# Attention iterations placed among the projections and the output projection of a hybrid encoder layer

## The chip, the cores and the metric

One Trainium2 chip; the kernel runs on one NeuronCore. The metric is the device time of one execution in microseconds. The kernel before takes 3338.55 us (median of three runs, 3337.0 to 3348.45).

## The reference

One encoder layer on x of 2048 tokens by 1024, all in fp32. Cut to what matters:

```python
h = rms_norm(x, norm1_g); proj = h @ w_in            # 1024 -> 2560
hy_in, q, k, v, pool_in = split(proj)                # 768, 512, 512, 512, 256
y_hy   = hyena_mixer(hy_in, ..., hyena_filter(...))  # long convolution, by DFTs
y_na   = neighbourhood_attention(q, k, v, na_rpb)    # 8 heads of 64, window 8 x 16 on a 32 x 64 grid
y_pool = pool_mixer(pool_in, pool_w, pool_scale)     # means over 2, 4, 8, 16 tokens
mixed  = concat(rms_norm(y_hy), rms_norm(y_na), rms_norm(y_pool)) # each with its part of mix_norm_g
x = x + mixed @ w_out
x = x + expert_choice_moe(rms_norm(x, norm2_g), w_router, w_gate, w_up, w_down)  # 16 experts, 256 tokens each
return rms_norm(x, final_g)
```

## The kernel before, in words

Everything is one class, `Trunk`; `run` strings the stages together. Large products are done in a reduced fp32 format, each as three matmuls: `split` cuts an operand into a high part (ScalarE, L212) and the rest (VectorE, L213), and `mm3` (L217 to L219) multiplies high by high, high by low and low by high. Tiles come from rotating pools: a tag with `bufs=n` has n buffers, and the next tile of that tag waits for the last reader of the one whose buffer it takes. A scheduler with a simulated timeline decides the order of the instructions on each engine; each engine then runs its own list strictly in order.

**Projections** (`proj`, `prep`, `slab`). The 2048 tokens are four chunks of 512, two chunks to a half. `prep` loads a tile of 128 tokens (`x0`, 4 buffers), takes the RMSNorm (ACT L236, POOL L204 and L206, DVE L238), transposes it on TensorE (L243, 8 transposes a tile) and splits it into `hT_h`, `hT_l`. The 2560 columns are ten slabs of 256, in five groups of two; slabs 0 to 2 feed the hyena mixer, 3 and 4 are queries, 5 and 6 keys, 7 and 8 values, 9 pooling. Each half runs all five groups over its two chunks: 80 calls of `slab`, 24 matmuls of 512 columns each (48 of 256 for values). Weights come in pieces of 512 KB on SP's queue. Results go to HBM (`Ud`, `KD`, `QD`, `Vd`).

**Beside the projections**: in the first half the generator `filt` (the filter of the hyena mixer, its DFT; POOL L392 and TensorE L395 among its lines) and `bias_tables`; in the second half `hyena` (39 steps, four a slab call) and `pooling` (eight steps, from the seventh slab call on, one a call). One pooling step is a chain: load `po<-Ud` (L557, POOL's queue), sums on DVE (L548) and POOL (L562, L567), scale (L570), one matmul (L577, PSUM tag `fl`), eviction (ACT L579) into the loaded tile, store `Ypd` (L580). Its three tiles take all three buffers of the tag, so the next load waits for this store.

**Attention** (`attention`) then has PSUM to itself (`psum_b`: two banks each of `s`, `tp`, `o`). It has 16 units of four iterations, 64 in all. An iteration is `scores` (6 matmuls `s<-at_k,at_q`; DVE L768 adds the bias and takes the minimum; ACT L772 the exponential), `turn` (transposes `tp<-ident,at_s`, evicted by ACT L790 or DVE L788 into `at_p`) and `weigh` (`o<-at_p,at_v`, evicted by ACT L808). All of its TensorE instructions are recorded at L715, in `pe`, which chains each to the one before, so that their order is written out by hand. `load_wo` runs beside it: 32 loads of 128 KB of the output weight on POOL's queue (L870, `wo_raw`, 2 buffers), each multiplied by the norm's gain and split (ACT L862, DVE L863).

**Output projection** (`mix`, `out_proj`, `route`): eight chunks of 256 tokens. `mix` loads the three mixers' outputs and splits them; for each tile of 128 tokens 48 matmuls of 512 columns, the sum with x (DVE L978 into `wo_x`, 3 buffers), 8 transposes (L983), the store to `Acc`, a squared sum (ACT L988) and the router's logits. **The rest** is `top_tokens` and `experts`, which the change leaves as they are.

Of the kernel before, what the change touches and what calls it, by code (L numbers as in the profile page):

```python
# [10 lines left out]
F = mybir.dt.float32  # L11
# [142 lines left out]
def _layouts(a):  # L154
# [19 lines left out]
    w = np.ascontiguousarray(a["w_in"][0].reshape(2, 4, 128, 10, 256).transpose(3, 0, 2, 1, 4))  # L174
# [9 lines left out]
class Trunk:  # L184
# [30 lines left out]
    def mm3(self, out, lh, ll, rh, rl, start, stop):  # L215
# [6 lines left out]
    def prep(self, pool, early, chunk, out):  # L222
# [6 lines left out]
        for t in range(4):  # L229
            xt = self.sb(early, [128, D], "x0", bufs=4)  # L230
            nc.sync.dma_start(xt, x[(chunk * 4 + t) * 128:(chunk * 4 + t + 1) * 128])
            if chunk + t == 0:
                nc.sync.dma_start(self.g1, _bc(self.i["norm1_g"], D))
# [15 lines left out]
    def proj(self, pool, early):  # L249

        nc, i = self.nc, self.i
        self.g1 = self.sb(early, [128, D], "g1", bufs=1)
        ht = {}
        for _ in self.prep(pool, early, 0, ht):
            pass
        groups = ((1, 2), (0, 9), (7, 8), (5, 6), (3, 4))
        for half, group in itertools.product(range(2), groups):
            if 3 in group:
                self.copy_values(half)
            w = {}  # L260
            for s in group:
                wh, wl = [], []
                for q in range(2):
                    raw = self.sb(pool, [128, 4, 256], "w1_r", bufs=2)
                    nc.sync.dma_start(raw, self.c["w_in_t"][s, q])
                    h = self.sb(pool, [128, 4, 256], "w1_h", R, bufs=4)
                    l = self.sb(pool, [128, 4, 256], "w1_l", R, bufs=4)
                    self.split(h, l, raw)
                    wh += [h[:, d] for d in range(4)]
                    wl += [l[:, d] for d in range(4)]  # L270
                w[s] = wh, wl
            for ch in range(2):
                chunk = half * 2 + ch
                ahead = None
                if group == groups[-1] and chunk == 1 or group == groups[0] and ch == 0:
                    ahead = self.prep(pool, early, chunk + 1, ht)
                for s, m in itertools.product(group, range(2)):
                    if ahead:
                        next(ahead)
                    self.slab(pool, s, m, chunk, *w[s], *ht[chunk])  # L280
                    yield half, s

    def copy_values(self, half):

        rows = slice(half * 16, half * 16 + 16)
        for k, (c0, k0, nk) in enumerate(self.CB):
            self.nc.gpsimd.dma_start(self.Vc[k][rows], self.Vd.rearrange("(r c) n -> r c n", c=64)[rows, k0:k0 + nk])

    def slab(self, pool, s, m, chunk, wh, wl, hh, hl):
# [3 lines left out]
        if s in (7, 8):  # L293
            for t2 in range(2):
                sl = slice((m * 2 + t2) * 128, (m * 2 + t2 + 1) * 128)
                for d in range(8):
                    self.mm3(pt[:, t2 * 256:(t2 + 1) * 256], hh[:, d, sl], hl[:, d, sl],
                             wh[d], wl[d], d == 0, d == 7)
# [4 lines left out]
            nc.scalar.dma_start(dst.rearrange("(a p) n -> p a n", p=128), ev)  # L303
            return
        for d in range(8):
            self.mm3(pt, wh[d][:, m * 128:(m + 1) * 128], wl[d][:, m * 128:(m + 1) * 128],
                     hh[:, d, :], hl[:, d, :], d == 0, d == 7)
# [20 lines left out]
        else:  # L328
# [3 lines left out]
            nc.scalar.dma_start(self.Ud[r0:r0 + 128, tok], ev)  # L332


    def filt(self, pool):
# [6 lines left out]
        nc.gpsimd.dma_start(self.d2, c["dft_2"])  # L342
        nc.gpsimd.dma_start(self.d2p, c["dft_2p"].bitcast(R))
# [54 lines left out]
        for g4 in range(8):  # L398
# [4 lines left out]
            for g2 in range(2):  # L403
                ph = self.bank("fl", (128, 2, 256))
                for e in range(2):
                    k, x = g2 * 2 + e, 0 if g4 + g2 + e else 1
                    self.mm3(ph[:, e, :], self.d2p[:, 0, x], self.d2p[:, 1, x], ah[:, k, :], at[:, k, :], True, True)
# [13 lines left out]
    def hyena(self, pool):  # L421
# [5 lines left out]
        nc.gpsimd.dma_start(ph, c["par_h"])  # L427
        sw = ph[:, 0:18].rearrange("p (t k) -> p t k", k=3)
# [42 lines left out]
        for g4 in range(8):  # L471
# [6 lines left out]
            for g2 in range(2):  # L478
# [3 lines left out]
                for e in range(2):  # L482
                    k, x = g2 * 2 + e, 2 if first[e] else 0
                    nc.tensor.matmul(pz[:, e, :], lhsT=self.d2[:, x], rhs=at[:, k, :], start=True, stop=True)
# [12 lines left out]
                for e in range(2):  # L497
                    x = 3 if first[e] else 1
                    nc.tensor.matmul(pb[:, e, :], lhsT=self.d2[:, x], rhs=y[:, e, :], start=True, stop=True)
# [142 lines left out]
    def attention(self, kpool, get_pool):  # L642
# [42 lines left out]
        def load_values(u):  # L685
# [4 lines left out]
            for cb in self.QB[g * 2:g * 2 + 2]:  # L690
# [3 lines left out]
                if g:  # L694
                    if rb == 0:
                        wide[cb] = kb([128, 8, 256], f"at_vw{cb}")
                        nc.sync.dma_start(wide[cb][:, 0:4], values(0, 4, 128))
                        nc.gpsimd.dma_start(wide[cb][:, 4:8], values(512, 4, 128))
# [11 lines left out]
        mark = nc.cur_bb.bb.instructions[-1]  # L710
        self.chain = None

        def pe(op, *args, **kw):

            ins = op(*args, **kw).ins  # L715
            if self.chain is not None:
                self.tc.add_manual_dep(ins, self.chain.name,
                                       mybir.DependencyInfo(mybir.DependencyClass.NoSync, mybir.DependencyReason.DATA),
                                       reason="order of the attention")
            self.chain = ins  # L720
# [4 lines left out]
        def begin(u):  # L725
# [11 lines left out]
            if u + 1 < len(units):  # L737
                w.tabs = dict(bias)
                with self.tc.issue_after(mark):
# [681 lines left out]
```

## Time and profile before

| | |
|---|---|
| profiled execution, own time | 3335.52 us |
| its span on the core | 3333.7 us |
| median of 3 runs (lowest, highest) | 3338.55 us (3337.0, 3348.45) |
| busy in the span: PE, DVE, ACT, POOL | 96%, 57%, 46%, 11% |
| projections, filter, hyena, pooling | 0 to 600 us |
| attention, load of the output weight | 600 to 860 us |
| output projection | 860 to 1077 us |
| choice of the tokens | 1077 to 1133 us |
| experts, final norm | 1133 us to the end |

PE is TensorE's matmuls, PEld its weight loads, DVE VectorE, ACT ScalarE, POOL GpSimd, SP SyncE. A row "L715 ... x416 | 69.7, 310 | 48.0 <-ACT" says: line, engine, operation, out<-in, count, busy us, mean ns of one, idle us of the engine just before, and what ended it. Matmuls overlap, so the mean of one is a latency; its cost on a full engine comes from counts in a stretch without idle time. The bounds of the stages are where TensorE's lines change over.

### The profile page before, as it was taken

What the parts mean: (1) busy time and instruction counts of PE and PEld (TensorE: products, weight loads), DVE (VectorE), ACT (ScalarE), POOL (GpSimd) and SP (SyncE); (2) the same over time, 40 slices, a digit from 0 to 9 for tenths busy, and PEclk for the clock granted to TensorE, in tenths of its full rate; (3) what the DMA queues carried; (4) which work ended last, traced back from release to release, by engine and by line L of the source; (5) the groups of instructions that cost most, each with busy time, mean ns of one, the idle gap of its engine ahead of it and who ended that gap; (6) DMA issues with size and microseconds to landing.
All of it is one profiled execution on the core that took longest, in us unless ns stands there. A gap on an engine that the chain in (4) does not pass through costs nothing.

```text
span 3333.7 us, 45008 instructions
## 1 busy us (share of the span) xinstructions
PE 3190.7 (96%) x18002; PEld 2690.7 (81%) x18002; DVE 1902.3 (57%) x2555; ACT 1518.9 (46%) x2004; POOL 363.5 (11%) x468
## 2 busy tenths in 40 slices
PE   8999999678999599999999999999999999999998
PEld 6887898456787488888888888888888888888886
DVE  5124557356676665565665655656556565565565
ACT  4124422366332355454454544545445445454464
POOL 2212212222111000000000000000000000000012
PEclk9999999888999699999999999999999999999999
DMA  6677687875553457666576665665656656666596
GB/s 223 213 258 233 204 307 267 229 199 155 169 165 130 138 193 212 196 200 203 198 208 200 198 203 195 210 202 194 211 193 204 202 197 209 195 192 203 188 299 231
DMA packets 421782, 685.50 MB, mean 206 GB/s; under 512 B 27378, under 2 KB 323042, under 8 KB 421190
## 3 DMA queue, kind: packets, MB, share of 16 engines
q1 hardware_dynamic: 362742, 530.74, 49.4%
q0 software_dynamic: 29552, 106.09, 11.0%
q10 hardware_dynamic: 29280, 45.81, 4.0%
q8 instruction: 141, 2.31, 0.3%
q14 instruction: 67, 0.55, 0.0%
HBM read 573.86 MB, written 119.03 MB: 208 GB/s over the span
## 4 chain that ended last, share of the span: by engine, by line
PE 86%; DMA 6%; issue 4%; DVE 2%; ACT 1%; SPq 1%; POOL 0%; POOLq 0%; ACTq 0%; DVEq 0%
PE mm L1193 27%; PE mm L1195 13%; PE mm L217 13%; PE mm L219 13%; PE mm L218 13%; DMA at_t<-Ce 2%; PE tp L1162 1%; DMA mo_xg<-Hr,mo_ix 1%; DMA wo_raw<-in_w_out 1%; DMA QD<-e 1%; PE tp L715 1%; PE o L715 1%; DMA at_q<-QD 0%; PE tp L395 0%; PE fl L521 0%
## 5 line engine op out<-in xcount | busy, mean ns | idle before, releaser
L1193 PE MATMUL mm<-mo_xx,mo_wh 128*128 128x512 f32 x4096 | 1446.3, 398 | 0.6 <-DVE mo_xx L213 0.6
L213 DVE TENSOR_TENSOR mo_wl<-mo_raw,mo_wh 128x2048 fp32r<-128x2048 f32 x384 | 879.7, 2291 | 790.3 <-ACT mo_wh L212 790.2
L1195 PE MATMUL mm<-mo_xx,mo_wl 128*128 128x256 f32 x4096 | 1151.7, 281 | 0.0
L212 ACT ACTIVATE mo_wh<-mo_raw 128x2048 fp32r<-128x2048 f32 x384 | 735.4, 1915 | 702.8 <-issue 323.4
L1193 PEld LDWEIGHTS mm<-mo_xx,mo_wh 128*128 128x128 f32 x4096 | 771.3, 188 | 185.2 <-DVE mo_xx L213 1.0
L1195 PEld LDWEIGHTS mm<-mo_xx,mo_wl 128*128 128x128 f32 x4096 | 775.5, 189 | 0.7
L218 PE MATMUL mm<-mo_wl,mo_hh 128*128 128x512 f32 x1024 | 398.4, 389 | 0.0
L217 PE MATMUL mm<-mo_wh,mo_hh 128*128 128x512 f32 x1024 | 398.1, 389 | 0.0
L219 PE MATMUL mm<-mo_wh,mo_hl 128*128 128x512 f32 x1024 | 396.0, 389 | 0.0
L219 PEld LDWEIGHTS mm<-mo_wh,mo_hl 128*128 128x128 f32 x1024 | 192.2, 188 | 40.2
L217 PEld LDWEIGHTS mm<-mo_wh,mo_hh 128*128 128x128 f32 x1024 | 192.2, 188 | 40.1
L218 PEld LDWEIGHTS mm<-mo_wl,mo_hh 128*128 128x128 f32 x1024 | 192.3, 188 | 39.3
L1226 POOL DMA_INDIRECT Acc<-mo_y,mo_ix x30 | 69.5, 2315 | 1395.3 <-ACT mo_y L1225 1279.0
L217 PE MATMUL mm<-hT_h,w_h 128*128 128x512 f32 x512 | 204.6, 402 | 2.1 <-ACT hT_h L212 2.1
L218 PE MATMUL mm<-hT_l,w_h 128*128 128x512 f32 x512 | 205.1, 401 | 0.0
L219 PE MATMUL mm<-hT_h,w_l 128*128 128x512 f32 x512 | 204.0, 398 | 0.0
L1201 ACT ACTIVATE mo_s<-mo_s 128x512 f32<-128x512 f32 x128 | 81.0, 633 | 235.8 <-DVE mo_s L1198 235.6
L1198 DVE TENSOR_TENSOR mo_s<-mo_s,mm 128x512 f32<-128x512 f32 x256 | 174.0, 680 | 0.0
L1197 ACT ACTIVATE mo_s<-mm 128x512 f32<-128x512 f32 x256 | 147.7, 577 | 0.0
L217 PEld LDWEIGHTS mm<-hT_h,w_h 128*128 128x128 f32 x512 | 96.0, 188 | 25.8 <-ACT hT_h L212 2.8
L218 PEld LDWEIGHTS mm<-hT_l,w_h 128*128 128x128 f32 x512 | 96.1, 188 | 25.4 <-issue 2.8
L212 ACT ACTIVATE mo_hh<-mo_s 128x512 fp32r<-128x512 f32 x128 | 79.9, 624 | 78.7 <-DVE mo_s L1202 78.7
(307 smaller groups left out, 3614.8 us busy)
## 6 DMA issues: line engine op xcount, KB each, us to landing
mo_raw<-in_w_gate SPq DMA_DIRECT2D x128, 1024.0 KB, 5.4
mo_raw<-in_w_up SPq DMA_DIRECT2D x128, 1024.0 KB
mo_raw<-in_w_down SPq DMA_DIRECT2D x128, 1024.0 KB, 4.9
w_r<-c_w_in_t SPq DMA_DIRECT2D x40, 512.0 KB, 7.2
x<-in_x SPq DMA_DIRECT2D x16, 512.0 KB, 9.8
Ud<-e ACTq DMA_DIRECT2D x32, 256.0 KB, 4.4
Hd<-t ACTq DMA_DIRECT2D x32, 256.0 KB, 6.0
t<-Hd SPq DMA_DIRECT2D x16, 512.0 KB, 7.0
```

Source lines behind the costliest of these rows:

```text
L212: self.nc.scalar.activation(hi, src, AF.Copy)
L213: self.nc.vector.tensor_tensor(lo, src, hi.bitcast(F), op=OP.subtract)
L217: mm(out, lhsT=lh, rhs=rh, start=start, stop=False)
L218: mm(out, lhsT=lh, rhs=rl, start=False, stop=False)
L219: mm(out, lhsT=ll, rhs=rh, start=False, stop=stop)
L715: ins = op(*args, **kw).ins
L1193: nc.tensor.matmul(pt[:, m].rearrange("p k t -> p (k t)"), lhsT=w[:, d, ms], rhs=xx[:, d].rearrange("p k t -> p (k t)"), start=d == 0, sto ...
L1195: nc.tensor.matmul(pt[:, m, 1], lhsT=wlo[:, d, ms], rhs=xx[:, d, 0], start=False, stop=d == 7)
L1197: nc.scalar.activation(a, pt[:, :, 1], AF.Copy)
L1198: nc.vector.tensor_tensor(a, a, pt[:, :, 0], op=OP.add)
L1201: nc.scalar.activation(s, s, AF.Silu)
L1226: nc.gpsimd.indirect_dma_start(out=self.Acc, out_offset=off, in_=y, in_offset=None, compute_op=OP.add)
```

## The change

The projections run in three **phases**: phase 0 takes four slabs (1, 2, 0, 9) of the second half, phase 1 all ten slabs of the first half, one slab at a time, phase 2 the other six (7, 5, 3, 8, 6, 4) of the second half. Chunks 2 and 3 are therefore normalised and transposed twice. Weight pieces are 256 KB; in phase 2 they come on POOL's queue. `filt` runs beside phase 0 and the first two slabs of phase 1, `hyena` beside phase 1 from slab 0 on, and `pooling` when `hyena`'s steps are used up.

In phase 2 the matmuls join attention's chain (`held`). A slab call gives the control back three times; from the 16th time on one or two attention steps go between two parts (57 parts, 85 of 130 steps). The other 45 steps (22 iterations) follow with `load_wo` (two steps of it for each attention step), and then with `mix` and `out_tiles` for one tile of 128 tokens after every sixth step. The last tiles go in pairs as before. Attention's PSUM is now one bank `s`, two `tp`, one `o`, two `mm`, one `x`; `weigh` goes ahead of `scores`. A tile of one has one buffer for each of its `mx_h`, `wo_hh`, `wo_x`.

```diff
     def mm3(self, out, lh, ll, rh, rl, start, stop, held=False):
         mm = self.nc.tensor.matmul
+        if held:
+            mm = lambda *a, **k: self.pe(self.nc.tensor.matmul, *a, **k)
...
+    PHASES = ((1, ((1, 2), (0, 9))),
+              (0, ((1,), (2,), (0,), (9,), (7,), (5,), (3,), (8,), (6,), (4,))),
+              (1, ((7,), (5,), (3,), (8,), (6,), (4,))))
...
+                    for q in range(4):
+                        raw = self.sb(wpool, [128, 2, 256], "w1_r", bufs=wbufs[0])
+                        (nc.gpsimd if ph == 2 else nc.sync).dma_start(raw, self.c["w_in_t"][s, q])
+                        h = self.sb(wpool, [128, 2, 256], "w1_h", R, bufs=wbufs[1])
...
+                        again = ph == 2 or ph == 1 and gi
+                        g1 = self.sb(late, [128, D], "g1", bufs=1) if again and ph == 1 else None
+                        ahead = self.prep(pool, late if again else early, ahead, ht, g1, 1 if again else 4)
...
                 for d in range(8):
                     self.mm3(pt[:, t2 * 256:(t2 + 1) * 256], hh[:, d, sl], hl[:, d, sl],
-                             wh[d], wl[d], d == 0, d == 7)
+                             wh[d], wl[d], d == 0, d == 7, held)
+                    if t2 * 8 + d in (4, 9):
+                        yield t2
...
+                if len(line) > 2:
+                    weigh(line.pop(0))
                 line.append(scores(unit, j, hp))
+                yield
                 if len(line) > 1:
                     turn(line[-2])
-                if len(line) > 2:
-                    weigh(line.pop(0))
                 yield
...
+                if ph == 1:
+                    if kpool is None and part == 2:
+                        more = steps(hy, 4)
+                        if n > 27:
+                            more = steps(side, 1) or more
...
+                    psa = psum("psum_b", s=1, tp=2, o=1, mm=2, x=1)
+                    at = self.attention(kpool, attn_pool)
+                    next(at)
+                    n = 0
+                if n > 15:
+                    for _ in range(1 + n % 2):
+                        next(at)
+            proj.release()
+            wo = sbuf("wo", left)
+            self.out_weights(wo)
+            weights = self.load_wo(wo)
...
+                if weights:
                     with tc.issue_after(self.mark_act), tc.issue_after(self.mark_dve):
-                        if n % 3 == 0:
-                            steps(wo, 1)
-                        if n == 54:
-                            ready = self.mix(pools["early"], 0, self.bank("o", (128, 2, 128))[:, 0])
+                        if not steps(weights, 2):
+                            weights = None
+                elif ready and n % 6 == 0:
+                    self.out_tiles(osmall, ready, "x", 1, 1)
+                    done, ready = done + 1, None
+                if not weights and not ready and done < self.tiles:
+                    ready = self.mix(osmall, done, 1, "x", 1)
...
+            while done < 16:
+                t0, nt = ready[0:2]
+                nxt = self.mix(opool, t0 + nt, 2, "s", 2) if t0 + nt < 16 else None
+                if nt == 1:
+                    self.out_tiles(osmall, ready, "o", 1, 1)
+                else:
+                    self.out_tiles(opool, ready, "o", 2, 2)
+                done, ready = t0 + nt, nxt
```

How it moves instructions, at three places. The rows are the instructions of one engine in the order in which it runs them: line, operation, out<-in, shape.

**TensorE, phase 2 of the change**: a slab of values with attention between its parts (`mm` is the projection, `s`, `tp`, `o` the three parts of an iteration). In the kernel before no projection stands among attention's rows.

```order
L217 MATMUL o_5703<-at_p_5612,at_vw_951_4765 64x128
L217 MATMUL o_5703<-at_p_5620,at_vw_951_4765 64x128
L217 MATMUL s_5712<-at_k_5378,at_q_5381 128x360 x6
L217 MATMUL tp_5726<-ident,at_s_5644 120x128 x3
L217 MATMUL tp_5732<-ident,at_s_5647 120x128 x3
L217 MATMUL mm_5687<-w_h_5543,hT_h_4154 128x256
L217 MATMUL mm_5687<-w_l_5544,hT_h_4154 128x256
L217 MATMUL mm_5687<-w_h_5543,hT_l_4155 128x256
```

Attention's matmuls and the projection's are now one written order, which TensorE keeps whatever is ready.

**TensorE, the pooling matmuls** (`fl<-po`). Before, one among the projection's (`mm`), in the second half:

```order
L218 MATMUL mm_4429<-w_l_3900,hT_h_2592 128x256
L219 MATMUL mm_4429<-w_h_3899,hT_l_2593 128x256
L217 MATMUL mm_4429<-w_h_3899,hT_h_2592 128x256
L577 MATMUL fl_3603<-po_656_3597,po_par_3362 128x512
L218 MATMUL mm_4429<-w_l_3900,hT_h_2592 128x256
L219 MATMUL mm_4429<-w_h_3899,hT_l_2593 128x256
```

In the change, between phase 1 and phase 2 (`tp<-ident,x` is the second preparation of chunk 2):

```order
L255 MATMUL tp_4257<-ident,x_857_4240 128x128 x4
L619 MATMUL fl_3277<-po_702_3271,po_par_3127 128x512
L255 MATMUL tp_4274<-ident,x_864_4264 128x128 x4
L255 MATMUL tp_4281<-ident,x_864_4264 128x128 x4
L619 MATMUL fl_3350<-po_721_3342,po_par_3127 128x512
L255 MATMUL tp_4359<-ident,x_888_4349 128x128 x4
L255 MATMUL tp_4366<-ident,x_888_4349 128x128 x4
L619 MATMUL fl_3393<-po_728_3387,po_par_3127 128x512
L255 MATMUL tp_4383<-ident,x_895_4373 128x128 x4
L255 MATMUL tp_4390<-ident,x_895_4373 128x128 x4
L619 MATMUL fl_3438<-po_735_3430,po_par_3127 128x512
L619 MATMUL fl_3485<-po_742_3476,po_par_3127 128x512
```

Before, the last seven of the eight pooling matmuls have 47 to 91 rows between neighbours, most of them projections. Now the last six, and the transposes of five tiles, stand in 16 rows without a projection; the next row of a projection is phase 2's first, in a PSUM pool that takes over the banks of `fl`.

**ScalarE, the splits of the output weight** (`wo_h<-wo_raw`). Before, amid attention's evictions (`at_o`, `at_p`) and exponentials (`at_s`):

```order
L772 ACTIVATE at_s_5848,at_sum_5708<-at_s_5848,at_min_5844 128x360
L862 ACTIVATE wo_h_5265<-wo_raw_5754,wo_gm_5263 128x256
L862 ACTIVATE wo_h_5265<-wo_raw_5756,wo_gm_5263 128x256
L808 ACTIVATE at_o_5707<-o_5830 128x16x16
L790 ACTIVATE at_p_5913<-tp_5909 120x384
L772 ACTIVATE at_s_5897,at_sum_5708<-at_s_5897,at_min_5896 128x480
L772 ACTIVATE at_s_5900,at_sum_5708<-at_s_5900,at_min_5896 128x480
L772 ACTIVATE at_s_5930,at_sum_5708<-at_s_5930,at_min_5929 128x480
```

In the change, the end of a run of 29 splits:

```order
L899 ACTIVATE wo_h_7175<-wo_raw_7413,wo_gm_7173 128x256
L899 ACTIVATE wo_h_7175<-wo_raw_7415,wo_gm_7173 128x256
L899 ACTIVATE wo_h_7175<-wo_raw_7421,wo_gm_7173 128x256
L899 ACTIVATE wo_h_7175<-wo_raw_7423,wo_gm_7173 128x256
L212 ACTIVATE wo_hh_1568_7553<-tp_7587 128x512
L212 ACTIVATE mx_h_7673<-mx_y_7676 128x256
L212 ACTIVATE mx_h_7673<-mx_y_7684 128x256
L1030 ACTIVATE wo_hr_7632,wo_ss_7633<-wo_x_7555 128x1024
L212 ACTIVATE wo_hh_1568_7553<-tp_7624 128x512
L212 ACTIVATE mx_h_7673<-mx_y_7705 128x256
L822 ACTIVATE at_p_7761<-tp_7756 128x384
L822 ACTIVATE at_p_7761<-tp_7756 96x128
```

Before, at most a few splits stand side by side. Now 29 of the 32 stand in one run, and the next eviction of attention's transposes (`at_p`) on ScalarE comes behind them.

## Rows read from the trace of the kernel before

**Rows 1.** Windows by stage: PE, PEld, DVE, ACT, POOL busy, clock, DMA share, GB/s.
```profile
0.00:600.00 600.00, 583.72 (x3099) 490.48 (x3100) 276.06 (x392) 199.68 (x313) 135.70 (x213) 1.00 0.74 245
600.00:860.00 260.00, 196.54 (x1708) 145.46 (x1707) 126.36 (x422) 140.47 (x433) 60.22 (x91) 0.84 0.70 185
860.00:1077.00 217.00, 215.25 (x1102) 174.23 (x1100) 154.26 (x283) 71.73 (x169) 33.29 (x62) 1.00 0.47 154
1077.00:1133.00 56.00, 15.62 (x117) 10.75 (x117) 39.50 (x170) 17.13 (x39) 4.14 (x2) 0.50 0.41 134
1133.00:3333.70 2200.70, 2179.54 (x11982) 1869.74 (x11980) 1306.15 (x1291) 1089.87 (x1050) 130.13 (x100) 0.99 0.64 204
```

**Rows 2.** Windows without idle time: projections of 512 columns; attention. PE busy, clock.
```profile
75.00:100.00 25.00, 25.00 (x113) 1.00 0.35 106
...
680.00:700.00 20.00, 20.00 (x210) 1.00 0.60 179
```

**Rows 3.** Groups of attention's TensorE instructions, 600 to 860 us.
```profile
L715 PE MATMUL tp<-ident,at_s 128*128 128x128 f32 (+3 forms) x416 | 69.7, 310 | 48.0 <-ACT at_s L772 25.1 <-DVE at_p L788 15.6 <-DVE at_min L768 3.5
L715 PE MATMUL s<-at_k,at_q 64*128 64x360 f32 (+5 forms) x384 | 55.1, 397 | 8.9 <-DMA at_q<-QD 8.9
L715 PE MATMUL o<-at_p,at_vw 128*64 128x128 f32 (+1 forms) x448 | 34.7, 300 | 0.0
L715 PE MATMUL o<-at_p,at_v 120*64 120x128 f32 (+2 forms) x384 | 32.7, 313 | 0.0
```

**Rows 4.** Waits of TensorE, 590 to 860 us: total, times, longest.
```profile
PE tp L715 <- ACT at_s L772: 25.1, 8, 9.2
PE tp L715 <- DVE at_p L788: 15.9, 4, 9.0
```

**Rows 5.** The pooling tiles: ns min/median/max, first and last start.
```profile
L557 POOL DMA_DIRECT2D po<-Ud x8: 537/546/594, 339.8 to 566.8; - x8
L548 DVE TENSOR_TENSOR po<-po x24: 689/700/1064, 347.1 to 581.8; 128x527 f32<-128x527 f32 x8, 64x512 f32<-64x512 f32 x8, 128x525 f32<-128x525 f32 x4, 128x521 f32<-128x521 f32 x4
L570 DVE SCALAR_TENSOR_TENSOR po<-po,po_e,po x8: 730/748/778, 350.0 to 584.6; 128x512 f32<-128x512 f32 x8
L577 PE MATMUL fl<-po,po_par x16: 590/592/667, 382.1 to 589.1; 128*128 128x512 f32 x16
L579 ACT ACTIVATE po<-fl,po_par x8: 687/687/691, 383.3 to 589.8; 128x512 f32<-128x512 f32 x8
```

**Rows 6.** DMA issues, 440 to 600 us: size, median us to landing.
```profile
Ypd<-po ACTq DMA_DIRECT2D x7, 256.0 KB, 2.0
po<-Ud POOLq DMA_DIRECT2D x3, 264.0 KB, 6.0
```

**Rows 7.** Timeline, eight transposes of one prepared tile: at the start; amid projections.
```profile
8.56 1.97 PE L243 MATMUL tp<-ident,x 128*128 128x128 f32 x8 [8.56 <-DVE x L238]
...
285.78 1.03 PE L243 MATMUL tp<-ident,x 128*128 128x128 f32 x8
```

**Rows 8.** The tile wo_raw: its loads and its two splits.
```profile
L870 POOL DMA_DIRECT2D wo_raw<-in_w_out x32: 536/539/599, 621.3 to 810.6; - x32
L862 ACT ACTIVATE wo_h<-wo_raw,wo_gm x32: 492/498/510, 646.3 to 817.3; 128x256 fp32r<-128x256 f32 x32
L863 DVE SCALAR_TENSOR_TENSOR wo_l<-wo_raw,wo_gm,wo_h x32: 471/480/1460, 646.8 to 819.5; 128x256 fp32r<-128x256 f32 x32
DMA to landing us min/median/max: 2.4/6.8/13.8
```

**Rows 9.** DMA issue in a quiet stretch, 683 to 684 us.
```profile
wo_raw<-in_w_out POOLq DMA_DIRECT2D x1, 128.0 KB, 2.8
```

**Rows 10.** The filter's sums on POOL: ns min/median/max.
```profile
L392 POOL TENSOR_TENSOR t<-t,t x16: 1275/1301/2275, 85.6 to 192.1; 128x512 f32<-128x512 f32 x16
```

**Rows 11.** The tile wo_x of the output projection.
```profile
L978 DVE SCALAR_TENSOR_TENSOR wo_x<-mm,rms_r,wo_x x96: 729/746/753, 856.4 to 1071.5; 128x512 f32<-128x512 f32 x96
L988 ACT ACTIVATE wo_hr<-wo_x x16: 1046/1057/1062, 865.1 to 1072.5; 128x1024 f32<-128x1024 f32 x16
```

More of the change, by code (lines that the diff above doesn't have):

```diff
@@ L219, in mm3, with prep @@
         mm(out, lhsT=ll, rhs=rh, start=False, stop=stop)
-    def prep(self, pool, early, chunk, out):
+    def prep(self, pool, early, chunk, out, g1, xbufs):
         nc = self.nc
@@ L247, in prep, with proj @@
             yield
-    def proj(self, pool, early):
-        nc, i = self.nc, self.i
-        self.g1 = self.sb(early, [128, D], "g1", bufs=1)
+    PHASES = ((1, ((1, 2), (0, 9))),
+              (0, ((1,), (2,), (0,), (9,), (7,), (5,), (3,), (8,), (6,), (4,))),
+              (1, ((7,), (5,), (3,), (8,), (6,), (4,))))
+    def proj(self, pool, early, sbuf):
+        nc = self.nc
         ht = {}
-        for _ in self.prep(pool, early, 0, ht):
-            pass
[L256 to L281, printed above, removed]
@@ L283, in copy_values @@
-    def copy_values(self, half):
-        rows = slice(half * 16, half * 16 + 16)
+        wpool, wbufs, late = sbuf("w_a", "left"), (4, 8), None
+        for _ in self.prep(pool, early, 2, ht, self.sb(early, [128, D], "g1", bufs=1), 4):
+            pass
+        for ph, (half, groups) in enumerate(self.PHASES):
+            if ph == 1:
+                wpool.release()
+                wpool, wbufs = sbuf("w_b", "left"), (4, 5)
+                late = sbuf("late", "left")
+            for gi, group in enumerate(groups):
+                w = {}
+                for s in group:
+                    wh, wl = [], []
+                    for q in range(4):
+                        raw = self.sb(wpool, [128, 2, 256], "w1_r", bufs=wbufs[0])
+                        (nc.gpsimd if ph == 2 else nc.sync).dma_start(raw, self.c["w_in_t"][s, q])
+                        h = self.sb(wpool, [128, 2, 256], "w1_h", R, bufs=wbufs[1])
+                        l = self.sb(wpool, [128, 2, 256], "w1_l", R, bufs=wbufs[1])
+                        self.split(h, l, raw)
+                        wh += [h[:, d] for d in range(2)]
+                        wl += [l[:, d] for d in range(2)]
+                    w[s] = wh, wl
+                for ch in range(2):
+                    chunk = half * 2 + ch
+                    ahead = None
+                    if gi == 0 and ch == 0:
+                        ahead = chunk + 1
+                    elif gi + 1 == len(groups) and ch == 1 and ph < 2:
+                        ahead = self.PHASES[ph + 1][0] * 2
+                    if ahead is not None:
+                        again = ph == 2 or ph == 1 and gi
+                        g1 = self.sb(late, [128, D], "g1", bufs=1) if again and ph == 1 else None
+                        ahead = self.prep(pool, late if again else early, ahead, ht, g1, 1 if again else 4)
+                    for s, m in itertools.product(group, range(2)):
+                        for _ in range(2 // len(group)):
+                            if ahead:
+                                next(ahead)
+                        if ahead and ph == 2 and m:
+                            late.release()
+                        for part in self.slab(pool, s, m, chunk, *w[s], *ht[chunk], ph == 2):
+                            yield ph, s, part
+                for s in group:
+                    if s in (7, 8):
+                        self.copy_values(half, s - 7)
@@ L286, in copy_values @@
+        wpool.release()
+    def copy_values(self, half, hg):
+        rows, cols = slice(half * 16, half * 16 + 16), slice(hg * 256, hg * 256 + 256)
         for k, (c0, k0, nk) in enumerate(self.CB):
-            self.nc.gpsimd.dma_start(self.Vc[k][rows], self.Vd.rearrange("(r c) n -> r c n", c=64)[rows, k0:k0 + nk])
-    def slab(self, pool, s, m, chunk, wh, wl, hh, hl):
+            self.nc.gpsimd.dma_start(self.Vc[k][rows, :, cols], self.Vd.rearrange("(r c) n -> r c n", c=64)[rows, k0:k0 + nk, cols])
@@ L291, in slab @@
+    def slab(self, pool, s, m, chunk, wh, wl, hh, hl, held):
         nc = self.nc
@@ L427, in hyena @@
         nc.gpsimd.dma_start(ph, c["par_h"])
+        d2 = sb([128, 4, 128], "d2")
+        nc.gpsimd.dma_start(d2, c["dft_2"])
         sw = ph[:, 0:18].rearrange("p (t k) -> p t k", k=3)
@@ L709, in attention @@
         pool = get_pool()
[L710 to L720, printed above, removed]
+        pe = self.pe
         class Pair:
@@ L738, in begin @@
                 w.tabs = dict(bias)
-                with self.tc.issue_after(mark):
-                    ahead = load(u + 1), load_values(u + 1)
+                ahead = load(u + 1), load_values(u + 1)
             w.nkr = self.RB[w.rb][2]
@@ L810, in weigh @@
                 finish(w)
+        self.tiles = 0
         def finish(w):
+            self.tiles = 4 * w.rb + 4 if w.hg else 0
             dst = self.Yad[w.hg * 256:w.hg * 256 + 256, w.rb * 512:w.rb * 512 + 512]
```

305 lines of the change are left out of this document (158 added, 147 removed).

## The prediction

> **What bounds the kernel now.** I read the windows by stage first [rows 1]: what share of each stage TensorE is busy, and at which clock. In four of the five stages it has next to nothing to give: 584 of 600 us in the projections, 215 of 217 in the output projection, 2180 of 2201 behind it, all at a clock of 0.99 or 1.00. The 56 us of choosing tokens are untouched. Only attention, 600 to 860 us, shows slack: 197 us busy of 260, at a mean clock of 0.84, so between the two levels of 1.2 and 2.4 GHz. The reader is to see there that 63 us are idle and that the busy part is stretched too. The groups and waits tell why: TensorE waits for the exponentials and evictions between the three parts of an iteration, 25.1 us on ScalarE's at_s, 15.9 on VectorE's at_p, in pieces of up to 9 us [rows 3, 4]. There is nothing else for it to do meanwhile.
>
> **What full speed would give.** In a stretch of projections without idle time 113 matmuls take 25 us, 0.221 each; in a stretch of attention without idle time, at clock 1.00, 210 take 20 us, 0.095 each [rows 2]. Attention has 416 + 384 + 448 + 384 = 1632 records [rows 3], 155 us. The stage's other 76 records (of 1708 [rows 1]) lie between these two prices, 12 us at the middle. So its TensorE work is 167 us, and 260 - 167 = **93 us** is the most that spreading it among projections and output projection can save.
>
> **What the change adds, part by part.**
>
> *Work.* Eight tiles are prepared a second time: at 1.03 us for eight transposes [rows 7], 8 us on TensorE. Its loads, sums and splits lie on the other engines, at most 57% busy over the span. The router's 64 more matmuls, narrower than before, I bound by nothing (narrower ones cost less) and 64 x 0.095 = 6; 4 taken. Sum **+12**.
>
> *From phase 0 to phase 1.* Four filter steps stand at the end without projections between them. The nearest row is the sum on POOL, 1.30 us, two a step [rows 10]: 4 x 2.6 = **+10**, from 0 if the filter runs ahead to 20 if each step also waits for its loads.
>
> *From phase 1 to phase 2: pooling.* TensorE's order puts six pooling matmuls and five tiles' transposes side by side, with no projection among them; phase 2's first matmul comes behind, in a PSUM pool that waits for pooling's banks. Pooling steps can't overlap, since the load needs the buffer that the store of the step before empties. One step: issue 0.55, three sums on DVE (24 in eight steps) of 0.70, scale 0.75, matmul 0.59, eviction 0.69 [rows 5], store 2.0 [rows 6]: 6.7 us, and the load. The load took 6.0 in the busy stretch [rows 6]; the shortest comparable one is 2.8, for 128 KB in a quiet stretch [rows 9]. A step is 9.5 to 12.7 us, six are 57 to 76. Nearest is the low end, because the projections' stores have stopped. What covers it is the transposes, 5 x 1.97 at the low clock [rows 7], 10 us, which run beside. So 57 - 10 = **+47**, from 25 (steps that start early, under the last projections) to 66. Before, the same steps lay under some 80 projection rows each and cost TensorE nothing; that cover is what is gone. Second late thing: five tiles come one by one through a single x0 buffer, but beside pooling, so I add nothing.
>
> *The output weight.* Before, its 32 loads were spread over 621 to 811 us beside attention. Now they can't start until the projections have given up their memory, and 29 of ScalarE's 32 splits stand in one run, ahead of attention's next evictions. Two buffers: per pair a landing, the split on ACT 0.50 and on DVE 0.48, and the issue's remainder, some 0.4 (0.54 less what lies beside) [rows 8]. Landings run from 2.4 by 6.8 to 13.8 us [rows 8], 2.8 in a quiet stretch [rows 9]; in a burst with little else moving I take 3.0. That is 4.4 us a pair, 14 pairs, 61 us; some seven iterations of attention (seven times 1632 / 64 x 0.095 = 2.4 us, 17 us) and the first matmuls of the output projection stand ahead, of which I count 10 as cover: **+51**, from 14 x 3.8 - 17 = 36 to 14 x 8.2 - 10 = 105 at the median landing. Here a rule can be held against the rows. The row's shortest landing is 2.4 us, its median nearly three times that, on a loaded DMA system. The Trainium skill, page "DMA: Bandwidth & Descriptors", section "Anatomy of one DMA - SWDGE (gpsimd) path", gives a fixed part of about 2.0 us and the bytes over 436 GB/s: 2.3 us for 128 KB. By it, as an estimate, a pair is 3.7 us, the run 52, and this term 42 instead of 51; the whole would come out 9 us lower. The measured 2.4 agrees with it as a floor and the 6.8 does not, so I stay with the rows. The same rule speaks against the smaller weight pieces and one-tile loads, each of which pays the fixed part again; these are fetched ahead, so that hits latency only where one buffer is left.
>
> *Tiles of one.* Eight tiles go singly, with one wo_x buffer each. Behind the last matmul come the sum 0.75, the square 1.06 [rows 11], the norm, the stores and the next load; a load or store of this kind is 2.0 to 6.0 us [rows 6]. That is about 12 us against 48 x 0.221 + 8 x 0.128 = 12 us of matmuls a tile, with attention between in six of them. So it hides narrowly: **+15**, some 2 us a tile, from 0 to 30.
>
> *The written order in phase 2.* Each attention matmul that is late now holds up projections behind it, and with one bank of s the next scores wait for VectorE. Between a score and its transposes the order has some 30 matmuls of the projection, 3 us even at half of 0.221 for the narrow ones, against two instructions each on DVE and ACT; the nearest rows of such a width are 0.48 and 0.50 [rows 8], so 2 us: covered. What isn't is a unit's first loads; bounds 0 and 15, **+5** taken. Weights one slab at a time give the splits less lead; within the same 15.
>
> **Sum.** -93 + 12 + 10 + 47 + 51 + 15 + 5 = +47. On the profiled execution's own time of 3335.5 (span 3333.7 and 1.8 around it) this is 3382.5; the median of the three runs lies 3 us above that execution, so I say **3386 us**. Experts and choice of tokens shift unchanged. The cases below count from the median too, 3338.5.
>
> **Rivals.**
> *Both chains run ahead (faster).* Place: the second boundary. If the pooling loads go out while the last projections still run, three or four of the six steps are over when TensorE arrives, and the term is 15; the same for the weight, if attention's iterations cover 30 us of it, 20. Then -93 + 12 + 15 + 20 + 10 = -36, 3303. For it: the chain is only loads and light engines, and before, TensorE is busy 584 of the 600 us in which they run [rows 1]. Against it: the three buffers of pooling allow no step ahead, and the weight's place isn't free earlier. It decides where the new stalls sum to less than 81 us (93 - 12).
> *One chain covered, one not (no change).* -93 + 12 + 47 + 30 = -4, 3335: say the weight's chain hides, and pooling's and the smaller stalls stay.
> *Loads land as in busy stretches (far slower).* With 6.0 for pooling and 6.8 for the weight: -93 + 12 + 66 + 105 + 30 = +120, 3459. For it: attention's first loads and the weights of phase 2 share the DMA system there (share 0.70 to 0.74 [rows 1]).
> *The written order isn't what runs.* Then attention stays a block and nothing is saved, 3350 or more with the added work. The order of TensorE's rows shows attention among projections, so I give it no chance of its own.
>
> **How the numbers follow.** Forecast 0.60, chains ahead 0.20, no change 0.13, far slower 0.07. A run of this kernel can tell about 0.5%, 17 us, from no change. The chance of faster is the second case, 0.20; same 0.13; slower 0.60 + 0.07 = 0.67. The range reaches from just under the faster case, 3295 (about half of it lies below), to just under the far slower one, 3455; it leaves out 0.10 and 0.04, and takes in the bounds of the terms above. The forecast's own range is 3345 to 3430.
>
> **What would show it.** Right: in attention's stretch a clock near 1.00 and no idle time among projections; before phase 2's first matmul 40 to 60 us in which TensorE waits for po tiles and x0; behind the last projection a stretch of about 50 us in which it waits for wo_h or at_p, while wo_raw lands one pair at a time. Wrong: pooling steps that start before the last projections end; weight loads that overlap attention; or, on the other side, TensorE waiting all through phase 2 for at_s or for weights, which I price at 5.

## The result and the profile after

The changed kernel takes **3514.38 us** (median of four runs, 3511.81 to 3521.05) against 3339.09 us, a ratio of 1.0522 with a 95% interval of 1.0497 to 1.0548: 175 us slower. The forecast was slower, 3386 us, with a range to 3455; the time lies above the range. The profiled execution of the change took 3521.05 us, 185.5 us more than that of before.

Windows by stage of the change (columns as in [rows 1]). The stages are: phases 0 and 1; the passage to phase 2; phase 2 with attention; the load of the output weight; tiles of one among attention's rest; pairs; choice of tokens; experts.

```profile
0.00:500.00 500.00, 460.54 (x2362) 381.37 (x2362) 246.81 (x344) 178.35 (x301) 122.78 (x192) 0.98 0.76 251
500.00:590.00 90.00, 41.33 (x184) 29.81 (x185) 36.92 (x55) 20.12 (x35) 18.18 (x32) 0.64 0.55 132
590.00:810.00 220.00, 217.13 (x1645) 172.24 (x1643) 91.21 (x297) 104.03 (x299) 42.00 (x62) 1.00 0.69 203
810.00:905.00 95.00, 37.15 (x223) 24.05 (x222) 33.61 (x92) 33.05 (x89) 26.60 (x44) 0.64 0.38 110
905.00:1147.00 242.00, 179.74 (x1014) 137.21 (x1012) 112.89 (x279) 75.41 (x219) 27.07 (x55) 0.78 0.32 98
1147.00:1265.00 118.00, 116.41 (x608) 94.11 (x608) 80.87 (x148) 36.84 (x88) 18.06 (x35) 1.00 0.43 138
1265.00:1319.00 54.00, 14.21 (x114) 9.37 (x114) 39.31 (x174) 15.70 (x38) 4.48 (x3) 0.52 0.42 139
1319.00:3519.30 2200.30, 2181.72 (x11992) 1871.35 (x11992) 1309.34 (x1296) 1091.31 (x1053) 126.78 (x100) 0.99 0.65 205
```

The experts take what they took. Up to there the change needs 1319 us, before 1133 [rows 1], 186 us more, and the rows say where. Idle time of TensorE was 16 + 63.5 + 2 us before the choice of tokens; now it is 39 (phases 0 and 1), 49 (passage), 3 (phase 2), 58 (weight), 62 (tiles of one) and 2 (pairs): 131 us more. Busy time, the choice of tokens included, rose from 1011 to 1066 us, 55 us, of which 12 are the added work of the prediction's first term, an estimate. The other 43, by subtraction, are the same matmuls at a lower clock, 0.64 in two of these stages and 0.78 in a third; that is a net sum, since most of attention's matmuls, at 0.84 before, now run at 1.00 in phase 2. 131 + 55 is the whole difference.

So the stretch that was to be filled is full: in phase 2 TensorE is busy 217 of 220 us at clock 1.00, with attention's instructions in it. The loss is in the stages around it. What TensorE waited for there (waits: total, times, longest), from 490, from 800 and from 900 us on:

```profile
PE tp L255 <- DVE x L250: 29.9, 6, 8.8
PE fl L619 <- DVE po L617: 12.7, 2, 6.8
PE fl L619 <- DVE po L612: 8.1, 3, 3.8
...
PE mm L228 <- ACT wo_h L899: 39.4, 6, 10.7
PE tp L217 <- ACT at_p L822: 15.5, 1, 15.5
...
PE mm L228 <- ACT mx_h L212: 28.7, 6, 7.3
PE mm L228 <- DVE wo_x L1020: 21.5, 11, 4.2
PE x L939 <- DVE mx_q L937: 7.9, 1, 7.9
```

In the passage it waits for both chains that the prediction looked at, tiles of x and pooling. In the weight's stage it waits for wo_h and for at_p, as the order of ScalarE had it. In the third it waits for the next tile's mx_h and for evictions into wo_x. The chain of work that ended last shows why; some of its pieces from 993 to 1033 us, in order of time: start, duration, what.

```profile
993.29 3.61 DMA mx_q<-Rd
...
996.90 1.50 issue
...
998.40 0.44 DVE mx_y L931
...
999.33 0.80 PE mm L228
...
1002.26 0.66 PE x L939 x4
...
1002.94 0.59 SPq L928
...
1003.57 4.09 DMA mx_q<-Rd
...
1007.79 0.43 DVE mx_y L931
1008.22 0.67 DVE wo_x L1020
...
1008.93 0.80 PE mm L228
...
1013.57 0.43 PE mm L230
...
1014.39 0.23 PE mm L229
...
1028.64 4.42 DMA mx_q<-Rd
```

One tile's turn is from one load of mx_q to the one in its place in the next turn, 1028.64 - 993.29 = 35 us. A tile has two such loads of 64 KB, and twice in a turn one stands in the chain, 3.6 to 4.4 us. At 993.29 it is the tile's own second load, and TensorE waits for the split of its product (mx_h). At 1003.57 it is the next tile's first one, issued right behind the norm matmul (L939) of this tile that frees a buffer. VectorE has the product that waits for it (1007.79) ahead of this tile's eviction into wo_x (1008.22), so that the eviction waits too. TensorE's work in such a turn is 48 x 0.221 + 8 x 0.128 for the tile and 6 x 1632 / 130 x 0.095 = 7 us of attention, 19 us in all. Of the 16 us lost some 7 are idle time. The rest is the clock: behind the wait of 4.0 us for mx_h it is granted at 0.50 (1.2 GHz) from 999 to 1013.5 us, at 1.00 from 1014.4 us on, and the tile's matmuls take 0.43 us each in the one stretch and 0.23 in the other.

### The profile page after: what moved, and what is told of

The parts are those of the page before. It is cut to its first block, busy times and chain, and to the rows that moved or that the text cites. A ratio compares the mean times of both kernels' runs of the same rounds, so it can differ in the third digit from the quotient of the medians.

```text
span 3519.3 us, 45782 instructions
## 1 busy us (share of the span) xinstructions
PE 3248.2 (92%) x18130; PEld 2719.5 (77%) x18130; DVE 1951.0 (55%) x2679; ACT 1554.8 (44%) x2120; POOL 386.0 (11%) x520
## 4 chain that ended last, share of the span: by engine, by line
PE 80%; DMA 8%; issue 3%; DVE 2%; ACT 1%; POOL 0%; SPq 0%; ACTq 0%; POOLq 0%; DVEq 0%
PE mm L1233 26%; PE mm L1235 13%; PE mm L228 10%; PE mm L230 10%; PE mm L229 10%; PE mm L217 3%; DMA mx_q<-Rd 2%; PE o L217 1%; PE tp L217 1%; PE s L217 1%; DMA wo_raw<-in_w_out 1%; PE tp L1202 1%; DMA x<-in_x 1%; DMA at_t<-Ce 1%; DMA at_v<-Vc 1%
## 5 line engine op out<-in xcount | busy, mean ns | idle before, releaser
L228 PE MATMUL mm<-wo_h,mx_h 128*128 128x512 f32 x256 | 120.0, 470 | 89.7 <-ACT wo_h L899 39.4
L228 PE MATMUL mm<-hT_h,w_h 128*128 128x512 f32 x384 | 153.8, 404 | 5.3 <-ACT hT_h L212 5.2
L230 PE MATMUL mm<-hT_h,w_l 128*128 128x512 f32 x384 | 153.6, 402 | 0.0
L229 PE MATMUL mm<-hT_l,w_h 128*128 128x512 f32 x384 | 153.6, 400 | 0.0
L228 PEld LDWEIGHTS mm<-wo_h,mx_h 128*128 128x128 f32 x256 | 54.9, 215 | 109.5 <-ACT wo_h L899 43.4
```

## The experiments

Each kernel is the change with the edit shown, unless another base is named. Times are medians, and differences are between medians; ratios are to the kernel before, on the same chip. A band is the range that an expectation names.

**Buffers of the mix.**

```diff
-                y = sb([128, 2, N], "mx_y", F, 2)
+                y = sb([128, 2, N], "mx_y", F, 3 if nt == 1 else 2)
-                sq = sb([128, 2, N], "mx_q", F, 2)
+                sq = sb([128, 2, N], "mx_q", F, 3 if nt == 1 else 2)
```

> Single tiles only: three buffers of mx_y and mx_q instead of two. Theory (the tiles of one cost some 100 us because the next tile's loads of mx_q wait for a buffer that TensorE's norm matmul frees in the middle of the tile before, and then land in 4 to 5 us; they are 53 us of the chain in 900 to 1150 us): 30 to 60 us less, about 3465. Rival (the single mx_h is what binds: its splits wait for the tile's last matmul whatever has been loaded): 0 to 10 us less, 3505 to 3515.

Measured 3487.78 us, ratio 1.0441 (1.0416 to 1.0466): 27 us less. Neither band; the wait for a buffer is part of the loss, not most of it.

**No tiles of one.** The branch with `out_tiles` in attention's loop is taken out, and the first mix is one of a pair, after attention.

```diff
-                elif ready and n % 6 == 0:
-                    self.out_tiles(osmall, ready, "x", 1, 1)
...
+            ready = self.mix(opool, 0, 2, "s", 2)
             while done < 16:
```

> Attention's rest runs without output projection between, then eight pairs as in the kernel before. Theory (tiles of one lose 100 us against their work): the 18 iterations behind the weight cost 4.06 us each as in the kernel before (260 / 64), 73 us, the pairs 217 us, so 290 us in the place of 360 us from 905 to 1265 us: 70 us less, about 3445. Rival (the tiles fill attention's gaps and the stretch is slow for another reason, such as the low clock behind the stop for the weight): no change or up to 20 us more, 3515 to 3535.

Measured 3389.18 us, ratio 1.0145 (1.0122 to 1.0169): 125 us less, far more than expected. Its windows show what was missed, attention's rest with the weight's load beside it, then the first pair, then the pairs:

```profile
810.00:880.00 70.00, 63.95 (x634) 46.17 (x632) 47.37 (x156) 52.84 (x158) 27.26 (x46) 0.98 0.52 147
880.00:925.00 45.00, 29.15 (x110) 22.68 (x111) 25.71 (x46) 16.95 (x38) 11.94 (x22) 0.77 0.58 167
925.00:1125.00 200.00, 199.37 (x1030) 161.99 (x1028) 141.70 (x259) 65.39 (x154) 30.78 (x58) 1.00 0.48 159
```

Attention's 45 remaining steps run in 70 us at clock 0.98, 64 of them busy, and they cover 20 of the weight's 32 splits; the other 12 follow until 915 us. The stop of 95 us is gone too, but for the 16 us of idle time from 880 us on (waits: 11.6 us for mx_h, 3.6 for wo_h). The weight's load alone had not been the stop: with the out tiles ahead of attention's next iterations in TensorE's order, everything behind them had waited for the whole weight. Without them ScalarE has no run of 29 splits; beside attention at most two stand side by side.

**Pooling early, and three x0 buffers**, each alone:

```diff
-              (0, ((1,), (2,), (0,), (9,), (7,), (5,), (3,), (8,), (6,), (4,))),
+              (0, ((1,), (2,), (9,), (0,), (7,), (5,), (3,), (8,), (6,), (4,))),
...
-                if hy is None and (ph == 0 or s in (1, 2)):
+                if hy is None and (ph == 0 or s in (1, 2, 9)):
...
-                        if n > 27:
+                        if n > 6:
                             more = steps(side, 1) or more
```

> Slab 9 goes ahead of slab 0 in phase 1 and pooling's steps are issued from its third call on, beside the hyena mixer; its matmuls then stand among phase 1's projections, and five tiles' transposes alone stand before phase 2. Theory of the prediction (pooling's chain sets the boundary): 40 to 50 us less, about 3470. Rival (the tiles of x through the single x0 buffer set it, 8 to 9 us each): five tiles still take 43 us, so 10 to 20 us less, about 3500.

Measured 3520.93 us, ratio 1.0538 (1.0515 to 1.0562): nothing gained, outside both bands.

```diff
-                        ahead = self.prep(pool, late if again else early, ahead, ht, g1, 1 if again else 4)
+                        ahead = self.prep(pool, late if again else early, ahead, ht, g1, 3 if again else 4)
```

> Three x0 buffers for the second preparation instead of one; the pooling matmuls still stand in a run before phase 2, seven of them. Theory (pooling's chain sets the boundary): no change, within 10 us. Rival (x0 sets it): 30 us less, about 3485.

Measured 3508.46 us, ratio 1.0494 (1.0467 to 1.0522): 6 us less. By each run's own expectation the other chain is the one that binds. TensorE's waits around the passage, first with pooling early, then with three x0 buffers:

```profile
PE tp L255 <- DVE x L250: 59.3, 4, 29.1
```

```profile
PE fl L619 <- DVE po L612: 26.9, 4, 9.0
PE fl L619 <- DVE po L617: 14.8, 2, 9.5
```

Each kernel waits almost only for the chain that was left, 59 and 42 us, where the change waits 51 us for the two. With pooling out of the way TensorE even waited 29 us for one tile of x. SP's DMA queue shows a part of that: the next load of x comes only when the single buffer is free, after the transposes that end at 541.3 us, and by then attention's first loads are ahead of it.

```profile
516.46 0.33 SPq L242 DMA_DIRECT2D x<-in_x  x1
...
520.86 21.78 SPq L746 DMA_DIRECT2D at_v<-Vc  x4
...
549.90 41.35 SPq L242 DMA_DIRECT2D x<-in_x  x4
```

The queue costs this load 9 us. The rest is its landing: in the chain it takes 16.85 us, while the DMA engines are busy for 0.67 of the time (550 to 567 us), and the load after it 3.38.

```profile
549.90 16.85 DMA x<-in_x
...
572.33 3.38 DMA x<-in_x
```

Attention's loads start at 517 us here, in the change at 568. So the run does not show what the tiles of x would cost without them.

Both together:

> Pooling's early issue and the three x0 buffers together, the rest as in the change. Theory (two chains of about the same length run side by side before phase 2, pooling's steps and the tiles of x, so that taking away one alone gave 0 and 6 us): 45 to 65 us less than the change, about 3460. Rival (what holds phase 2 is something else that both kernels kept, such as attention's first loads or the weights on POOL's queue): 0 to 15 us less, about 3505.

Measured 3470.59 us, ratio 1.0377 (1.0341 to 1.0413): 44 us less than the change (48 by the ratios), at the lower edge of the band, 45, and clear of the rival's. The passage's window is now 77 us busy of 90, where it was 41:

```profile
500.00:590.00 90.00, 77.23 (x496) 63.79 (x495) 46.38 (x97) 34.24 (x78) 23.19 (x37) 0.91 0.83 241
```

**Everything but the tiles of one**: the edits of the second, third and fourth runs.

> The same two and no tiles of one. If the losses lie in different stretches they add: 125 us and the gain of the run before, 55, below the change's 3514: about 3335, no change from the kernel before. If attention in phase 2 now meets its first loads earlier, up to 20 us are given back: 3355.

Measured 3341.23 us, ratio 0.9994 (0.9978 to 1.001). The losses add, and with them taken out the rest of the change is even with the kernel before: up to the end of the output projection its idle time sums to 79 us, before to 82, but half of it now lies in phases 0 and 1. Its windows (phases 0 and 1, passage, phase 2, attention's rest, output projection):

```profile
0.00:500.00 500.00, 461.50 (x2315) 380.20 (x2316) 250.27 (x353) 183.36 (x310) 132.38 (x204) 0.97 0.78 253
500.00:590.00 90.00, 76.48 (x490) 63.53 (x489) 44.99 (x95) 33.65 (x78) 23.27 (x36) 0.89 0.84 235
590.00:775.00 185.00, 185.00 (x1468) 145.68 (x1469) 79.31 (x266) 90.52 (x268) 38.57 (x54) 1.00 0.65 197
775.00:860.00 85.00, 63.56 (x568) 46.23 (x565) 48.29 (x148) 53.43 (x152) 26.30 (x47) 0.86 0.51 152
860.00:1085.00 225.00, 219.71 (x1106) 177.98 (x1105) 158.62 (x285) 75.18 (x177) 36.12 (x67) 0.98 0.49 156
```

**With eight wo_raw buffers** (`"wo_raw", F, 2` becomes `8`) on that:

> As the run before with eight wo_raw buffers instead of two. Theory (with two buffers each pair of loads waits for the splits of the pair before, and about 16 us of TensorE's time at the end of attention are lost to that): 10 to 20 us less than the run before, about 3322, faster than the kernel before. Rival (attention covers the loads, and the loss there is the first mix): 0 to 5 us less.

Measured 3335.1 us, ratio 0.997 (0.9956 to 0.9985): 6 us less, between the two bands, and 0.3% under the kernel before. Its ten times reach from 3328.44 to 3344.52 us.

**Two wo_x buffers** besides the three of mx_y and mx_q:

```diff
-                    self.out_tiles(osmall, ready, "x", 1, 1)
+                    self.out_tiles(osmall, ready, "x", 2, 1)
```

> Tiles of one with three buffers of mx_y and mx_q as in the first run, and two of wo_x; to make room the norm's gain is left out, the normalised rows are multiplied by themselves instead. Theory (the one wo_x buffer, from the last sum over the store to the next load, is what binds once mx_q doesn't: TensorE waited 33 us for wo_x): 20 to 35 us less than the first run, about 3460. Rival (mx_h is next): 0 to 10 us less, about 3483.

Measured 3477.56 us, ratio 1.0391 (1.0358 to 1.0423): 10 us less than the first run by the medians, 17 by the ratios, so at the rival's edge or between the bands. TensorE still waits for evictions into wo_x as long as in the first run (32.8 us):

```profile
PE mm L228 <- DVE wo_x L1018: 32.2, 9, 8.9
```

So these waits are not for a buffer of wo_x. In most turns they are VectorE's order: the norm factor is ready at 1044.3 us, but the eviction stands behind a product of the next tile's mix (L931), and that waits for its load of mx_q.

```profile
1043.46 0.86 POOL L206 TENSOR_TENSOR rms_r<-rms_a,mhalf 128x3 f32<-128x3 f32 x1
...
1047.77 0.43 DVE L931 TENSOR_TENSOR mx_y<-mx_y,mx_q 128x256 f32<-128x256 f32 x1 [4.54 <-DMA mx_q<-Rd]
1048.12 0.74 DVE L1018 SCALAR_TENSOR_TENSOR wo_x<-mm,rms_r,wo_x 128x512 f32<-128x512 f32 x1
```

The one wo_x buffer, the only thing that the prediction priced in these tiles, is worth 10 to 17 us of the 100.

**Mix one tile ahead**, for tiles of one:

```diff
-                if not weights and not ready and done < self.tiles:
-                    ready = self.mix(osmall, done, 1, "x", 1)
+                if not weights and len(ready) < 2 and done + len(ready) < self.tiles:
+                    ready.append(self.mix(osmall, done + len(ready), 1, "x", 2))
```

> Tiles of one with the mix issued one tile ahead, two buffers of mx_h and mx_l; to make room the rows that the experts read are stored without norm and gain. Theory (between two tiles stand only six attention steps, some 7 us, and the mix, loads of mx_y and mx_q, splits, norm, takes 15 to 20 us and can't start before the tile ahead has freed mx_h, so most of it is exposed): 50 to 80 us less than the change, 3435 to 3465. Rival (the one wo_x buffer and the low clock make the loss): at most the 27 us of the first run, 3485 or more.

Measured 3449.51 us, ratio 1.0323 (1.0307 to 1.0339): 65 us less, in the theory's band. The stage of the tiles of one takes 190 us where it took 242, at clock 0.94 instead of 0.78; its bounds are a little further on in the work, with 1069 matmuls for 1014:

```profile
905.00:1095.00 190.00, 170.76 (x1069) 129.58 (x1068) 104.08 (x273) 75.00 (x219) 28.16 (x56) 0.94 0.47 132
```

A little of it is VectorE's work that the edit leaves out, 1.28 us a tile. The edit moves the mix ahead and gives it the buffers for that; the run does not tell the two apart.

**Seven wo_raw buffers** in the change as it is:

> Seven wo_raw buffers in the change as it is, tiles of one kept; for room the norm's gain is left out, rows are multiplied by themselves. Theory (the stop from 850 to 905 us is the loads two by two, each pair a landing and two splits): the 29 splits in a run then take 29 x 0.5 = 15 us and a landing, so 30 to 45 us less than the change, 3470 to 3485. Rival (what holds the run is not the loads but the order, attention's evictions behind all splits): under 10 us less.

Measured 3483.98 us, ratio 1.0431 (1.0415 to 1.0448): 30 us less, the edge of the theory's band. The loads, first the change, then this run (count, ns, first and last start in us):

```profile
L907 POOL DMA_DIRECT2D wo_raw<-in_w_out x32: 536/536/630, 834.2 to 907.2; - x32
```

```profile
L907 POOL DMA_DIRECT2D wo_raw<-in_w_out x32: 538/539/596, 830.5 to 870.0; - x32
```

32 loads in 73 us became 32 in 40. In the change, the loads of the stop land quickly (DMA issues, 850 to 905 us: size, median us to landing):

```profile
wo_raw<-in_w_out POOLq DMA_DIRECT2D x27, 128.0 KB, 2.4
```

**Early first mix**, on the run with eight buffers and without tiles of one: `mix(osmall, 0, 2, "x", 1)` after the 24th of attention's remaining steps.

> The eight-buffer run without tiles of one, and the first mix issued amid attention's rest, as the kernel before does. It takes away the 10 us in which TensorE waited for mx_h: about 3325, 0.4 to 0.7% under the kernel before. Rival (the mix's instructions on ScalarE and VectorE delay attention by as much): 3335.

Measured 3341.33 us, ratio 0.9999 (0.999 to 1.0008): 6 us more than the run that it builds on. A miss. TensorE's wait for mx_h, 10.1 us in that run's trace, is gone, and it waits 8.8 us at once for at_p from ScalarE, which speaks for the rival. But that trace is of the slowest of the run's ten executions, and why nothing is gained stays open.

**A longer phase 0**, on that:

```diff
-    PHASES = ((1, ((1, 2), (0, 9))),
+    PHASES = ((1, ((1, 2), (0, 9), (7, 5))),
...
-              (1, ((7,), (5,), (3,), (8,), (6,), (4,))))
+              (1, ((3,), (8,), (6,), (4,))))
...
-                if n > 15:
+                if n > 5:
```

> The run before (e12: early pooling, three x0 buffers, eight wo_raw buffers, no tiles of one, early first mix) with slabs 7 and 5 moved from phase 2 to phase 0, and attention from the sixth part of phase 2 on (67 steps there instead of 85). Theory (filter and hyena mixer need more projections over them than phases 0 and 1 give: 0 to 575 us lose about 55 us more to idle time and low clock than the same stretch of the kernel before): 8 more slab calls there, 42 us of projections, take back 15 to 25 us, and the 18 attention steps that move behind phase 2 cost 18 x (1.49 - 1.19) = 5 us: about 3325. Rival (the filter's own order, not its cover, makes the loss): 3340 to 3350.

Measured 3358.3 us, ratio 1.0056 (1.0042 to 1.007): 17 us more. A miss too. Attention now starts with less projection around it, and TensorE waits 28 us for its scores' bank and for queries (waits from 500 to 900 us), in the run before 6 for the bank and 5 for keys:

```profile
PE s L217 <- DVE at_min L800: 18.4, 5, 6.3
PE s L217 <- DMA at_q<-QD: 9.7, 2, 6.2
```

Idle time up to 500 us fell only from 38 to 32 us. What more cover would give phases 0 and 1 was therefore not told apart from this.

## Why the prediction came out as it did

**The side was right, and so was its kind of reason**: attention fills, and new stops cost more than it saves. Every sign that it named for being right came: a full phase 2, the wait before it for po and x, the wait for wo_h and at_p. None of these signs looked at the tiles of one, and there one term of the sum was mis-sized by far; the others were off by less.

**The tiles of one, "+15, some 2 us a tile, from 0 to 30", are the step that failed.** The stage lost some 100 us, an estimate: 62 are idle, and TensorE was busy for 180 at clock 0.78 where seven turns of 19 us are 133. The term weighed the turnaround of the one wo_x buffer against the tile's matmuls and left out the mix of the next tile: two loads of mx_q, each held until a norm matmul frees its buffer, products, splits, norm, with a single mx_h that the tile's last matmuls free and only six attention steps, 7 us, to cover it; and on VectorE that mix's product holds up the eviction of the tile before. In the kernel before the mix runs one chunk ahead and hides: TensorE is busy for 215 of 217 us [rows 1]. Shown by three runs: two wo_x buffers gave 10 to 17 us, more buffers of mx_y and mx_q 27, the mix one tile ahead 65. With this term near 100 the sum is some 3470, past the range's upper end; no rival had it. Of the 43 us from there to the measured time some 20 are idle time above the terms, most of it up to 500 us; the rest is taken to be the clock at the other stops, which no term held.

**The output weight, "+51, from 36 to 105"**, had the right place and size: 58 us idle, at clock 0.64. Of the two causes in it only the loads were priced. Seven buffers took back 30 us, so the loads two by two are about half; leaving out the tiles, whose matmuls need all of the weight and stand ahead of attention's rest, freed most of the rest too. For the landing 3.0 us were taken from the rows of before, and 2.4 measured. The Trainium skill, page "DMA: Bandwidth & Descriptors", section "Anatomy of one DMA - SWDGE (gpsimd) path", gives a fixed part of about 2.0 us and the bytes over 436 GB/s, which is 2.3 us for 128 KB as an estimate. The trace agrees, with 2.4 us in this stop, where the DMA share is 0.26 (850 to 905 us); the 3.0 was the worse guide.

**Pooling, "+47, from 25 to 66"**, was sized right: 49 us idle, and 44 us back when both chains were gone. "Second late thing: five tiles come one by one through a single x0 buffer, but beside pooling, so I add nothing" was right for the sum, but it hid that the tiles of x are about as long a chain: with pooling early nothing was gained, in part because attention's loads then met those of x, and with three x0 buffers 6 us.

**"From phase 0 to phase 1", "+10, from 0 to 20"**, was low: 39 us idle up to 500 us, before 16 in the same 500, and clock 0.98. The place was right for half of the 23 us more: 12 us lie between 150 and 200 us, where the filter's matmuls (fl) stand without projections and TensorE waits for its tiles. The longest of these waits:

```profile
PE fl L228 <- ACT t L212: 4.6, 1, 4.6
```

Another 5 us are one wait for hT_h at 59 us. Why the filter runs that late isn't settled; the longer phase 0 didn't help.

**The written order in phase 2, "+5 taken"**, held: 3 us idle in 220.

**The 93 us, "the most that spreading it among projections and output projection can save"**, stand as an upper end: no run came out more than 0.3% under the kernel before. But the clock wasn't followed through: a new stop also slows the matmuls that stand in and behind it, 43 us net over all stages. The terms for the stops were idle time alone. The forecast's 0.67 for slower was borne out; the rival in which loads land slowly was not what made it so, since the weight's landed faster.

## What to carry to other kernels

Before a step is moved under new cover, list every chain that feeds its next turn, with each wait for a buffer and the engine that frees it, and compare the whole turn with the cover between two turns; here 35 us stood against 19. Read the order on the engines beside TensorE too: a product that waits for a load held up an eviction that was ready. Where two chains of about the same length end at one point, taking away either gains next to nothing, and only both together show their price. Here, without the tiles of one and without the stops at the passage and at the weight, the change came out even with the kernel before or 0.3% under it. That filling an idle stage pays only if the stages that lent the work keep enough over their own side chains is argued from the idle time in phases 0 and 1, not shown: the one run that gave them more cover lost elsewhere.

## What the runs showed beyond that

A load of 512 KB took part in a 29 us wait behind attention's first loads, though its data was needed first: 9 us by its place in SP's queue, and some 13 by landing in 16.85 us where the next such load took 3.38. And stops cost more than themselves: TensorE's clock was 0.64 over the two stages with stops of about 50 us, and still 0.78 in the third, where single waits were 8 us at most.
